# A third place for forward states, output scales in half the steps, a later last transpose and earlier latent norms in a hybrid retention and attention layer

## The chip, the cores and the metric

The kernel runs on one core of one Trainium2 chip. A core has TensorE (PE, matmuls and transposes into PSUM), VectorE (DVE), ScalarE (ACT), GpSimd (POOL) and SyncE (SP, which here issues nearly all DMAs). Each engine works through its own instructions in order and waits on semaphores for the others. The metric is the time of one execution in microseconds (us) on the device; lower is better. Before the change it was 2648.01 us, the median of three runs (2645.45 to 2649.12).

## The reference

One layer of a diffusion transformer over 2048 latent tokens of width 1024 and 256 context tokens, all in float32. What is computed, cut to what matters:

```python
h  = modulate(rmsnorm(x, norm1_g), sh1, sc1)           # latents
hc = modulate(rmsnorm(ctx, norm1_g), csh1, csc1)       # context
rq, rk, rv, rg, aq, ak, av = split(h @ w_in)           # 2816 columns
s_f, s_b = final states of the context's keys and values, forward and backward
# retention: 4 heads of 128, chunks of 128 tokens, both directions
state = state * c_dec + (k * k_dec).T @ v              # from chunk to chunk
ret = group_norm(o_forward + o_backward) * gn_g * silu(rg)
# attention: 8 query heads over 2 key heads of 64, keys of context and latents
att = softmax(q @ k.T / 8) @ v
x = x + g1 * (concat(ret, att) @ w_out)
h2 = modulate(rmsnorm(x, norm2_g), sh2, sc2)
x = x + g2 * (square(relu(h2 @ w_ff1)) @ w_ff2)        # hidden width 4096
return rmsnorm(x, final_norm_g)
```

## The kernel before, in words

Every float32 product is made of three half-precision products: each operand is split into a high and a low part ("hi", "lo"; ScalarE makes the high part, VectorE or GpSimd subtracts it), and hi times hi, hi times lo and lo times hi are summed in PSUM. The kernel has three stages, and in each of them the order of the instructions on every engine is written out by hand.

**Projections** (to about 604 us). The work is a list of units, one for each block of columns of w_in and each token tile (128 tokens): 24 matmuls (lines 1192 to 1194) into one of five PSUM tiles of the pool psO. Everything else is put beside the units with `do(step, part, function)`: after the matmuls of unit s, `run_step(s)` issues the functions put at step s, in the order of PARTS (hi, evac, turned, low, vec, pool, root, aux, turn, load, store). The evacuation of unit s - 1 stands in part evac of step s. Group 0 of the tiles is the context and four latent tiles; the other twelve latent tiles (group 1) are read and normalised beside the units of group 0. Each such tile has a step b: its load (line 450) is at b - 4, its square with a sum along the row (line 457, ScalarE) at b - 2, the root of the mean (lines 461 and 462, GpSimd) at b - 1, the multiplication by the root (norm, line 466, VectorE) and the eight transposes (line 480, TensorE, into two tiles of the PSUM pool psT, which has two) at b. The scaling that reads them (line 485, VectorE) and the shift (line 489, GpSimd) are at b + 1, the high part (line 492) at b + 2, the low part (line 495) at b + 3. The tile's place in SBUF is one of six and is free after the low part. L541 is the low part of a weight block. The first unit of the block RV has the step 20, so b runs from 23 to 28 and from 30 to 35.

**Attention and retention** (about 604 to 1485 us). Step k of `on(k, phase, function)` runs the phases begin, scores, piece, maximum, early, exp, cast, low, chain, pe, values, late, dma. For each step TensorE makes one tile of scores (line 210), one piece of the row maxima's scores (line 177 or 181, two PSUM tiles; VectorE reduces them at line 190 one step later) and some of the products with the values (lines 243 and 245). Beside it run the retention and, one tile of 128 tokens after the other from the last to the first, the output projection. `retention(26)` first takes the forward state from chunk 12 on: for each of five chunks a product of weighted keys and values (line 1633, two steps; GpSimd weighs the keys at line 1627, both operands are loaded ahead by SyncE) and an update of the state (line 1643, VectorE, in phase late). Each state goes to DRAM by line 1648. The states are written to tiles with the tag "sf", of which there are two; the backward states that follow have the tag "sb", of which there are two as well. `output_scales(39)` makes the scales of the output projection: a maximum over a column (VectorE), a transpose (TensorE), a maximum, a product that spreads it over the partitions (TensorE), and nine small VectorE operations, one list entry at each of eight steps in phase late. They set gns (read at the roots of the retention's group norm from step 53 on), sco and inv (read from step 67 on).

**Feed-forward** (from about 1485 us). One level of Strassen's scheme makes seven products do for eight, of sums and differences of blocks; an item is one of the seven: twelve matmuls (lines 2071 to 2073) into a PSUM tile from a ring of six tiles, evacuated by VectorE (line 2083) or ScalarE (line 2093). The last output tile (tokens 0 to 127) is finished at the join of the stages: x1 is stored (line 1850), normalised in place by GpSimd (`norm`, line 1860), transposed (line 1865, eight transposes into the two banks of psX), modulated by VectorE (line 1870), shifted by GpSimd (line 1875) and stored as h2 (line 1878). From `transpose_x` on these eight calls lie in the list `rest`, and the loop over items at the end takes two of them after the matmuls of each item, from the first item on. When the list is empty, psX is closed and its two banks join the ring as its next two tiles. In this join the seven h forms (line 2061), and raw weights (line 2030) are loaded; sums of weights are made by GpSimd (line 2042), their high and low parts by ScalarE (line 2047) and VectorE (line 2053).

Of the kernel before, what the change touches and what calls it, by code (L numbers as in the profile page):

```python
# [41 lines left out]
STATES = 12  # L42
# [14 lines left out]
def layer_kernel(ctx: ExitStack, tc: tile.TileContext, a: dict, out: bass.AP):  # L57
# [70 lines left out]
    def binade(x):  # L128

        nc.vector.tensor_scalar_max(x, x, 1e-15)  # L130
        nc.vector.tensor_single_scalar(x.bitcast(I32), x.bitcast(I32), 0x7F800000, op=ALU.bitwise_and)
# [17 lines left out]
    class Group:  # L149
# [52 lines left out]
        def turn(self):  # L202
            for i in range(0, P, 32):
                nc.vector.transpose(self.qr[64:96, 1, :, i : i + 32], self.mt[i : i + 32])
# [65 lines left out]
    with ExitStack() as st, tc.manual_schedule():  # L270
# [36 lines left out]
        def do(s, part, fn, *args):  # L307
            steps.setdefault((s, part), []).append((fn, args))
# [188 lines left out]
        def new_h(g, kind, i):  # L497
            if g == 0:
                return [hp.tile([P, KT, P], F32R, name=f"h{v}_{kind}{i}", tag="h") for v in ("hi", "lo")]
            h = hp.tile([P, 2, KT, P], F16, name=f"h_{kind}{i}", tag="h")  # L500
            return [h[:, 0], h[:, 1]]
# [705 lines left out]
        for (g, col), w in weights.items():  # L1207
            s = first[g, col]
# [3 lines left out]
            for j in range(w.n):  # L1212
                f, h = s - 5 + j, s - 3 + j if j < 2 else s - 1
                if (g, col) == (0, C_AQ):
                    f, h = s - 7 + j, s - 4 + j
                if (g, col) == (1, C_RQ):
                    f, h = s - 9 + j, (s - 6, s - 5, s - 2, s - 2)[j]
                f, h = f - early_by, h - early_by
# [3 lines left out]
        for n, (col, s) in enumerate(((C_RK, 5), (C_AKV, 6), (C_AQ, 12), (C_RQ, 16), (C_RV, 18), (C_RG, 26))):  # L1222
            w = weights[0, col]
            for j in range(w.n):
                at = s + (j if col != C_RV else j > 0)
                to = 1536 + 4 * n if col != C_RG else 1560
# [5 lines left out]
        for n, tile_of in enumerate(GROUPS[1]):  # L1232
            b = first[0, C_RV] + 3 + n + n // 6
            rows, x = Rows([tile_of], 1), {}

            def turn(n=n, rows=rows, x=x):
                kind, i = GROUPS[1][n]
                hs[1, n] = new_h(1, kind, i)
                x["p"] = [Part(kind, rows.x[0], hs[1, n], k, 4) for k in (0, 4)]
                for p in x["p"]:  # L1240
                    p.turn()

            def each(what, x=x):
                for p in x["p"]:
                    getattr(p, what)()

            do(b - 4, "load", rows.load, 0)
            do(b - 2, "hi", rows.square, 0)
            do(b - 1, "hi", rows.root)
            do(b, "vec", rows.norm, 0)  # L1250
            do(b, "turn", turn)
            do(b + 1, "vec", each, "scale")
            do(b + 1, "pool", each, "shift")
            do(b + 2, "hi", each, "high")
            do(b + 3, "low", each, "low")
# [15 lines left out]
        s = first[1, C_RG]  # L1271
# [222 lines left out]
        s = len(units)  # L1494
# [9 lines left out]
    def pool(stack, name, bufs=1, **kw):  # L1504
        return stack.enter_context(tc.tile_pool(name=name, bufs=bufs, reuse_waits="tile", **kw))
# [23 lines left out]
    def bank(i, shape=(P, 4, P)):  # L1529
        return psX.tile(list(shape), F32, name=f"bank{i}", tag=f"bank{i}")  # L1530
# [3 lines left out]
    def on(k, phase, fn, *args):  # L1534
        events.setdefault((k, phase), []).append((fn, args))

    def run(k, phase):
        for fn, args in events.pop((k, phase), ()):
            fn(*args)
# [4 lines left out]
    def link():  # L1544
        if chain:
            chain.pop(0)()
# [63 lines left out]
    def retention(k0):  # L1610
# [94 lines left out]
        for n, (d, c) in enumerate(todo):  # L1705
            k = k0 + SF * n
            on(k - 7, "dma", take, c, "rk")
            on(k - 5, "dma", take, c, "rv")
            on(k - 3, "late", weigh, d, c)
            on(k, "pe", product, c, n % 2, (0, 1))  # L1710
            on(k + 1, "pe", product, c, n % 2, (2, 3))
            if d == 0:
                old, to, tag = ("f" if c == STATES else "s", c - 2), ("s", c - 1), "sf"
            else:
                old, to, tag = None if c == 1 else ("b", NT), ("b", NT - 1 + c), "sb"
            on(k + 1, "late", update, d, c, old, to, tag, (0, 1))
            on(k + 2, "late", update, d, c, old, to, tag, (2, 3))
            if d == 0:
                on(k + 2, "dma", keep_state, c - 1)
        assert k0 + SF * len(todo) <= R0  # L1720
        for n in range(NT):
            c, k = NT - 1 - n, R0 + RF * n
# [24 lines left out]
    rest = []  # L1747

    def rest_steps(n):
        for _ in range(min(n, len(rest))):  # L1750
            fn, *args = rest.pop(0)
            fn(*args)
# [6 lines left out]
    def output_scales(k):  # L1759

        x = {}

        def greatest():
            w = vp.tile([P, P + 4], F32, name="os")
            x["y"], x["t"], x["one"], x["m"] = w[:, :1], w[:, 1:2], w[:1, 4 : 4 + P], w[:1, 2:3]
            nc.vector.memset(x["one"], 1.0)
            nc.vector.tensor_reduce(x["y"], wmx[:, 72:], axis=AX.X, op=ALU.max, apply_absolute_value=True)

        def turn():
            x["ps"] = bank(1)  # L1770
            nc.tensor.transpose(x["ps"][:1, 0], x["y"], ident)

        def whole():
            nc.vector.tensor_reduce(x["m"], x["ps"][:1, 0], axis=AX.X, op=ALU.max)

        def spread():
            x["ps"] = bank(1)
            mm(x["ps"][:, 0, :1], x["one"], x["m"], start=True, stop=True)

        def scales():  # L1780
            y, t, mul = x["y"], x["t"], nc.vector.tensor_scalar_mul
            later = [
                lambda: nc.vector.tensor_copy(y, x["ps"][:, 0, :1]),
                lambda: binade(y),
                lambda: nc.vector.tensor_scalar(y, y, 2.0**-10, inv, op0=ALU.mult, op1=ALU.max),
                lambda: mul(gns[:, 0:1], y, y),
                lambda: mul(gns[:, 1:2], gns[:, 0:1], EPS),
                lambda: mul(sco, sci[:, 7:8], y),
                lambda: nc.vector.reciprocal(t, y),
                lambda: mul(inv, inv, t),  # L1790
            ]
            for i, fn in enumerate(later):
                on(k + 4 + i, "late", fn)

        on(k, "early", greatest)
        on(k + 1, "pe", turn)
        on(k + 2, "early", whole)
        on(k + 3, "pe", spread)
        on(k + 3, "late", scales)
# [153 lines left out]

    done = attention()
    retention(26)
    output_weights(30)
    output_scales(39)
    for n, t in enumerate(range(NT - 1, -1, -1)):
        made_at = output_tile(t, R0 + RF * n, n == NT - 1)
    for j in range(4):  # L1960
# [264 lines left out]
    def up_jobs():  # L2225

        first = {}
        for j, (n, i, hf) in enumerate(JOBS):
            first.setdefault((n, i), j)
            for k in range(4):  # L2230
                on(j, "pe", up_part, n, i, hf, k)
            on(j, "out", up_out, j, n, i, hf)
        for n in range(len(ITEMS) - 1):
            for i in range(7):
                if (n, i) in first:
                    at = first[n, i] + len(ITEMS[n][1]) - 1
                    on(at, "hi", hi_w1, n + 1, i)
                    on(at + 1, "lo", lo_w1, n + 1, i)
            on(first.get((n, 0), 0), "dma", fetch_w1, n + 2)
            if n > 0:  # L2240
                for i in range(2):
                    on(first[n - 1, 5 + i], "sum", sum_w1, n + 1, i)
                    on(first[n, i], "sum", sum_w1, n + 1, 2 + i)
        on(0, "late", lambda: last3[0](0))
        on(20, "late", lambda: nc.scalar.activation(ff["fg"], ff["fg"], AF.Copy, scale=float(D) ** 0.5))
        for j in range(4):
            h_forms(5 + 10 * j, j)
        first1 = first[AHEAD, 0]
        for m, b in enumerate(PLACE):
            w2_forms(first1 + 1 + (8 * m if m < 14 else 11 * m - 32), b)  # L2250
        for i in range(7):
            on(first[NB, 0] + 2 + 2 * i, "dma", fetch_w2, 0, i)
# [155 lines left out]
    with tc.manual_schedule():  # L2408
        for k in range(min(events)[0], max(events)[0] + 1):
            for phase in PHASES:  # L2410
                run(k, phase)
                if phase in ("maximum", "low", "late"):
                    link()
        assert not events and not chain
        up_jobs()
        down_jobs()
        k = min(events)[0]
        while events:
            for phase in FPHASES:
                run(k, phase)  # L2420
                if phase == "pe" and rest:
                    rest_steps(2)
                    if not rest:
                        banks.close()
                        ff["ps"].extend(pool(late_ff, "fp3", space=PSUM), "p", 2)
            k += 1
# [60 lines left out]
```

## Time and profile before

| what | us |
|---|---|
| median of three runs | 2648.01 |
| the profiled execution, whole | 2648.93 |
| its span, first to last instruction | 2647.1 |
| TensorE busy in the span | 2597.4 |
| VectorE busy | 2048.4 |
| GpSimd busy | 1756.4 |
| ScalarE busy | 1504.0 |
| mean granted clock of TensorE | 0.997 |

A line of a timeline has the start and the duration in us, the engine, the line of the kernel, the operation, what it writes and reads, and the number of instructions merged; in brackets stands how long the engine sat idle before it and what ended that. "SPq" is SyncE's queue of DMA issues. In the lists of waits the three numbers are the sum in us, the number of waits and the longest. A line of the windows has the stretch, its length, the busy time of each engine with its instructions, the clock that TensorE was granted (1.00 is full speed), the share of the DMA engines and GB/s. A line of the chain of waits has only start, duration and what it was. Matmuls are pipelined: their durations overlap, and one of 0.38 us is followed by the next after 0.22 us.

### The profile page before, as it was taken

The numbers are of one execution on the slowest core, as the hardware profiler recorded it, in microseconds if no ns is written. First come the engines' busy times: TensorE is split into PE (matmuls) and PEld (weight loads), VectorE is DVE, ScalarE is ACT, GpSimd is POOL, SyncE is SP. The second block draws the span as 40 slices with busy tenths as digits, with TensorE's granted clock in tenths as the row PEclk, the third lists the DMA queues.
The fourth block names the chain that finished last, engine by engine and source line by source line (L and its number), as shares of the span: only waits on it lengthen the run. The fifth ranks groups of instructions, "written<-read, shape, count | busy, mean of one in ns | idle before, by whom it ended". The sixth has DMA issues, their size and how long they took to land.

```text
span 2647.1 us, 45439 instructions
## 1 busy us (share of the span) xinstructions
PE 2597.4 (98%) x16617; PEld 1452.3 (55%) x16617; DVE 2048.4 (77%) x3098; ACT 1504.0 (57%) x2544; POOL 1756.4 (66%) x1451
## 2 busy tenths in 40 slices
PE   8999999998999999999999999999999999999998
PEld 5875555545666666666666444444444444444443
DVE  5788898667888888888887697889886656656686
ACT  3855343426877777888788576666665322222243
POOL 3644566545676668798887685677662666666686
PEclk9999999999999999999999999999999999999999
DMA  7876999737112123333322755777685757475453
GB/s 235 270 253 211 309 325 322 261 116 221 51 57 73 57 85 100 95 85 107 112 81 77 278 160 151 236 237 230 211 291 148 278 174 296 163 288 178 157 189 113
DMA packets 332903, 481.84 MB, mean 182 GB/s; under 512 B 90228, under 2 KB 200068, under 8 KB 328200
## 3 DMA queue, kind: packets, MB, share of 16 engines
q1 hardware_dynamic: 332664, 478.94, 54.9%
q8 instruction: 130, 2.13, 0.3%
q14 instruction: 93, 0.76, 0.1%
q10 hardware_dynamic: 16, 0.01, 0.0%
HBM read 321.89 MB, written 156.38 MB: 181 GB/s over the span
## 4 chain that ended last, share of the span: by engine, by line
PE 82%; DVE 6%; DMA 4%; ACT 4%; issue 2%; POOL 2%; SPq 0%; ACTq 0%; DVEq 0%; POOLq 0%
PE pd L2298 7%; PE pd L2300 7%; PE pd L2299 7%; PE pu L2071 7%; PE pu L2073 7%; PE pu L2072 7%; PE st L210 4%; PE o L245 4%; PE st L211 4%; PE pso L1193 4%; PE pso L1192 4%; PE pso L1194 4%; PE mp L177 3%; PE o L243 2%; PE bank L1835 2%; PE bank L1833 2%
## 5 line engine op out<-in xcount | busy, mean ns | idle before, releaser
L190 DVE TENSOR_REDUCE nm<-mp 128x1 f32<-128x512 f32 x558 | 377.5, 685 | 88.6 <-PE mp L177 82.9
L216 ACT ACTIVATE p<-st 128x512 f32<-128x512 f32 x576 | 341.4, 600 | 158.4 <-PE st L211 154.8
L227 POOL TENSOR_TENSOR plo<-p,phi 128x1024 f16<-128x1024 f32 x160 | 347.7, 2178 | 84.9 <-ACT phi L220 84.8
L2071 PE MATMUL pu<-hf,w1f 128*128 128x512 f16 x896 | 339.8, 379 | 0.6 <-DVE u L1870 0.6
L2072 PE MATMUL pu<-hf,w1f 128*128 128x512 f16 x896 | 339.8, 379 | 0.0
L2073 PE MATMUL pu<-hf,w1f 128*128 128x512 f16 x896 | 339.8, 379 | 0.0
L2298 PE MATMUL pd<-w,uf 128*128 128x512 f16 x896 | 339.6, 379 | 0.0
L2299 PE MATMUL pd<-w,uf 128*128 128x512 f16 x896 | 339.6, 379 | 0.0
L2300 PE MATMUL pd<-w,uf 128*128 128x512 f16 x896 | 339.6, 379 | 0.0
L2318 POOL TENSOR_TENSOR y<-y,d 128x512 f32<-128x512 f32 x128 | 210.4, 1646 | 146.9 <-ACT uf L2287 100.1
L220 ACT ACTIVATE phi<-p 128x1024 f16<-128x1024 f32 x288 | 305.2, 1060 | 0.0
L229 DVE TENSOR_TENSOR plo<-p,phi 128x512 f16<-128x512 f32 x256 | 237.6, 929 | 21.8 <-ACT phi L220 9.4
L243 PE MATMUL o<-wv,plo 128*128 128x65 f16 x2304 | 230.6, 193 | 0.0
L245 PE MATMUL o<-wv,phi 128*128 128x129 f16 x2176 | 228.9, 220 | 0.0
L210 PE MATMUL st<-qr,ks 128*128 128x512 f16 x576 | 218.3, 379 | 10.3 <-ACT p L216 7.9
L243 PEld LDWEIGHTS <-plo 128*128 128x128 f16 x2304 | 205.5, 98 | 29.3 <-issue 1.5
L2310 DVE SCALAR_TENSOR_TENSOR y<-pd,scy,y 128x512 f32<-128x512 f32 x160 | 116.8, 747 | 131.5 <-PE pd L2300 131.5
L211 PE MATMUL st<-qr,ks 128*128 128x512 f16 x576 | 218.5, 379 | 0.0
L2083 DVE TENSOR_TENSOR r<-pu,r 128x512 f32<-128x512 f32 x224 | 149.9, 683 | 82.8 <-PE pu L2073 57.7
L1192 PE MATMUL pso<-wf,h_l 128*128 128x512 f16 (+1 forms) x576 | 208.1, 361 | 0.0
L1194 PE MATMUL pso<-wf,h_l 128*128 128x512 f16 (+1 forms) x576 | 208.1, 361 | 0.0
L1193 PE MATMUL pso<-wf,h_l 128*128 128x512 f16 (+1 forms) x576 | 208.1, 361 | 0.0
(392 smaller groups left out, 6110.4 us busy)
## 6 DMA issues: line engine op xcount, KB each, us to landing
wm<-in_w_ff SPq DMA_DIRECT2D x64, 512.0 KB, 7.1
u<-r SPq DMA_DIRECT2D x128, 256.0 KB, 4.5
ur<-u SPq DMA_DIRECT2D x128, 256.0 KB, 5.8
y<-x SPq DMA_DIRECT2D x64, 512.0 KB, 6.0
wf<-w2f SPq DMA_DIRECT2D x112, 256.0 KB, 3.0
w<-wf SPq DMA_DIRECT2D x28, 1024.0 KB, 10.2
w1r<-in_w_ff SPq DMA_DIRECT2D x48, 512.0 KB, 5.4
x<-y SPq DMA_DIRECT2D x48, 512.0 KB, 2.6
```

The costliest lines, as they stand in the source:

```text
L190: nc.vector.tensor_reduce(dst, src, axis=AX.X, op=ALU.max, negate=True)
L211: mm(ps, ks2[:, self.g, k], q[:, 1], start=False, stop=True)
L216: nc.scalar.activation(self.p[kt // 2][:, kt % 2], self.s.pop(kt), AF.Exp, scale=HD**-0.5)
L227: nc.gpsimd.tensor_tensor(lo, p, hi, op=ALU.subtract)
L243: mm(o[:, : HD + 1], lo[:, i, c], v[:, : HD + 1], start=False, stop=False)
L245: mm(o, hi[:, i, c], v[:, :VW], start=False, stop=last)
L2071: mm(pu[hf, i], whi, hi, start=k == 0, stop=False)
L2072: mm(pu[hf, i], whi, lo, start=False, stop=False)
L2073: mm(pu[hf, i], wlo, hi, start=False, stop=k == 3)
L2298: mm(ps, u[:, 0, b], w[:, b, 0], start=b == 0, stop=False)
L2299: mm(ps, u[:, 0, b], w[:, b, 1], start=False, stop=False)
L2300: mm(ps, u[:, 1, b], w[:, b, 0], start=False, stop=b == 3)
```

## The change

Four places are edited; no operation is added or taken away.

- The twelve latent tiles of group 1: square, root and norm each come one step sooner (b - 3, b - 2, b - 1); load and transposes stay.
- The third of the five forward states (n == 2) is written to a tile with the tag "sb" instead of "sf".
- The output scales start at step 38 instead of 39, and their eight list entries of small operations stand two to a step.
- The calls in `rest` for the last output tile start after the matmuls of the third item (k == 2) instead of the first. So the transposes, the modulation, the shift and the store all come two items later, and so does the joining of the two banks to the ring.

```diff
-            do(b - 2, "hi", rows.square, 0)
-            do(b - 1, "hi", rows.root)
-            do(b, "vec", rows.norm, 0)
+            do(b - 3, "hi", rows.square, 0)
+            do(b - 2, "hi", rows.root)
+            do(b - 1, "vec", rows.norm, 0)
             do(b, "turn", turn)
...
             if d == 0:
-                old, to, tag = ("f" if c == STATES else "s", c - 2), ("s", c - 1), "sf"
+                old, to, tag = ("f" if c == STATES else "s", c - 2), ("s", c - 1), "sb" if n == 2 else "sf"
...
             for i, fn in enumerate(later):
-                on(k + 4 + i, "late", fn)
+                on(k + 4 + i // 2, "late", fn)
...
-    output_scales(39)
+    output_scales(38)
...
                 run(k, phase)
-                if phase == "pe" and rest:
+                if phase == "pe" and rest and k > 1:
                     rest_steps(2)
                     if not rest:
                         banks.close()
```

## The prediction

> **What bounds the kernel now.** I read the page's busy times first, then TensorE's own waits, then the windows with their clock, then the timelines around the longest waits and the chain of waits there.
>
> ```profile
> PE 2597.4 (98%) x16617; PEld 1452.3 (55%) x16617; DVE 2048.4 (77%) x3098; ACT 1504.0 (57%) x2544; POOL 1756.4 (66%) x1451
> ```
>
> TensorE is busy for 98% of 2647.1 us. The change takes no matmul away, so it can only win TensorE's idle 49.7 us (2647.1 - 2597.4) and stretches in which its clock is low.
>
> ```profile
> PE bank L1865 <- POOL xr L1860: 3.1, 1, 3.1
> PE mp L181 <- DVE wmx L190: 2.7, 1, 2.7
> ...
> PE psx L480 <- DVE x_l L466: 2.2, 2, 2.0
> PE psx L711 <- ACT sq L659: 2.1, 1, 2.1
> ...
> PE mp L177 <- DVE wmx L190: 0.6, 1, 0.6
> PE pu L2071 <- DVE u L1870: 0.6, 1, 0.6
> ```
>
> The columns are the sum, the number of waits and the longest. The three waits of 2.0 to 3.1 us each stand where one edit acts: L480 is the latents' transposes, L181 (with 0.6 at L177) waits for maxima that stand behind the state updates on VectorE, L1865 is the last tile's transposes, with 0.6 behind them at L2071. Next, the windows: length, busy time of each engine, then the granted clock.
>
> ```profile
> 180.00:200.00 20.00, 19.26 (x90) 16.21 (x91) 18.12 (x20) 15.69 (x26) 12.93 (x13) 0.91 0.49 159
> 360.00:380.00 20.00, 16.07 (x93) 8.72 (x92) 15.94 (x23) 8.22 (x14) 8.52 (x12) 1.00 0.94 319
> ...
> 620.00:640.00 20.00, 16.70 (x150) 12.00 (x148) 16.72 (x36) 10.76 (x17) 14.38 (x13) 0.91 0.82 263
> ```
>
> ```profile
> 1450.00:1500.00 50.00, 44.72 (x272) 23.07 (x271) 21.28 (x30) 20.82 (x38) 27.18 (x26) 0.97 0.73 274
> ```
>
> The clock falls in these three windows with 0.91, 0.91 and 0.97, and the three waits lie in them. It costs 0.09 x 20 = 1.8, again 1.8, and 0.03 x 50 = 1.5 us. The window at 360, with the wait of 2.1 us at L711, keeps 1.00. So a wait of two to three microseconds may, but need not, cost nearly its own length again:
>
> ```profile
> 178.35 0.39 PE L1194 MATMUL pso<-whi,hlo_l 128*128 128x512 f32 x1
> 180.74 1.48 PE L480 MATMUL psx<-ident,x_l 128*128 128x128 f32 x8 [2.00 <-DVE x_l L466]
> ...
> 184.15 0.63 PE L1194 MATMUL pso<-whi,hlo_l 128*128 128x512 f32 x1
> ...
> 188.07 0.39 PE L1192 MATMUL pso<-whi,hhi_l 128*128 128x512 f32 x1
> ```
>
> After the wait a matmul takes 0.63 us, later 0.39. What the three places lose in all: 2.0 + 1.8 = 3.8 (latents), 0.6 + 2.75 + 1.8 = 5.15 (states), 3.1 + 0.6 + 1.5 = 5.2 (last tile); 14.2 us is the most the change can win.
>
> [...]
>
> **The change part by part.**
>
> *Latents a unit sooner.* In each of 12 tiles a square (ScalarE), two small root operations (GpSimd) and one norm (VectorE) move one unit ahead; no DMA moves. The third tile decides:
>
> ```profile
> 174.76 3.50 DVE L541 TENSOR_TENSOR wlo<-wst,whi 128x1024 fp32r<-128x1024 f32 x3 [6.09 <-PE pso L1194]
> 178.18 1.28 DVE L485 TENSOR_TENSOR x_l<-psx,a 128x512 f32<-128x512 f32 x2
> 179.38 1.22 DVE L466 TENSOR_SCALAR x_l<-x_l,xy 128x1024 f32<-128x1024 f32 x1
> ```
>
> VectorE sits idle for 6.09 us, then takes three weight splits, two scalings (L485) and the norm, and TensorE starts at 180.74, 2.00 us late. One unit sooner the norm of 1.2 us falls into that idle stretch. What is late next are the two scalings: they free the two PSUM tiles (psT has two) that the transposes write, and they end at 178.8 and 179.46, where TensorE is ready at 178.7 (178.35 + 0.39). The first four transposes take some 0.4 us (estimate, half of the slow eight's 1.48 at full clock), so about 0.6 us of wait is left. The fourth tile's norm takes the vacated place, so nothing behind it moves. Gain 3.8 - 0.6 = 3.2 us. Ends: 1.4 if the clock falls in any case, 3.8 if nothing is left. The square's load stays where it is, so ScalarE may now wait for it, with evacuations queued behind; priced as a rival.
>
> *Third place.* No instruction is added.
>
> ```profile
> 617.66 0.61 DVE L1643 SCALAR_TENSOR_TENSOR sf<-sf,cd,bank 128x128 f32<-128x128 f32 x2 [1.63 <-DMA sf<-sf]
> ...
> 623.45 0.60 DVE L1643 SCALAR_TENSOR_TENSOR sf<-sf,cd,bank 128x128 f32<-128x128 f32 x2 [1.54 <-DMA sf<-sf]
> ...
> 627.39 0.61 DVE L1643 SCALAR_TENSOR_TENSOR sf<-sf,cd,bank 128x128 f32<-128x128 f32 x2 [1.62 <-DMA sf<-sf]
> ```
>
> The third, fourth and fifth update each wait for the store of the state two before them; behind them on VectorE stand the maxima for which TensorE waits. With "sb" for the third, the first of these waits goes, and the fourth finds its place (stored by 617.66) free. The fifth now needs the second state's place, whose store landed at 623.45. So VectorE reaches the fifth update at 623.45 instead of 627.39: 3.9 us sooner. The "sb" place comes back for the second backward state, by when its store has long landed. What is late on TensorE next is the load of the sixth product's v:
>
> ```profile
> 620.87 0.38 SPq L1619 DMA_DIRECT2D orv<-rv  x1
> ```
>
> ```profile
> 626.73 1.04 POOL L1627 TENSOR_TENSOR okw<-ork,kd 128x512 f32<-128x512 f32 x1 [2.85 <-DMA ork<-rk]
> ```
>
> ```profile
> 624.71 0.38 PE L181 MATMUL mp<-ks,qr 128*128 128x256 f16 x2 [2.75 <-DVE wmx L190]
> ...
> 628.32 0.65 PE L1633 MATMUL bank<-orv,okw 128*128 128x128 f32 x4
> ```
>
> The load behind it in the queue landed at 626.73; one transfer of 256 KB earlier, this one lands at about 625.8 (estimate). TensorE took that product at 628.32, so it wins only 2.5 us here. VectorE's lead of 3.9 us then takes some of the next wait, 1.16 us at 642.68 (row below): I take 0.7. Gain 3.2 us; ends 1.0 (loads later still, or the clock falls in the new wait of about 2 us) and 5.15.
>
> *Output scales.* The first operations come one step sooner, the nine small ones of VectorE that follow in four steps, not eight. Nobody waits for them: the first root that reads gns comes eight steps later, the first part scaled by inv some twenty. But they now stand ahead of a late maximum:
>
> ```profile
> 641.88 0.15 DVE L1783 COPY os<-bank 128x1 f32<-128x1 f32 x1
> ```
>
> ```profile
> 642.68 0.38 PE L177 MATMUL mp<-ks,qr 128*128 128x512 f16 x1 [1.16 <-DVE nm L190]
> ```
>
> One of them (0.15 us) stood ahead of it, now five: up to 0.6 us if VectorE is still behind, nothing if the third place has put it ahead. I take 0.3 us of loss.
>
> *Last tile's transposes.* Eight transposes pass two items (24 matmuls), two modulations pass four or five operations on VectorE, two shifts pass a sum on GpSimd, two stores pass loads on SyncE (read back some thirty items later), and the two freed banks join the ring two items later.
>
> ```profile
> 1474.17 13.37 DMA x<-xr
> 1487.80 1.10 POOL xr L1860
> ...
> 1500.29 0.22 PE pu L2072
> ```
>
> ```profile
> 1488.96 1.97 PE L1865 MATMUL bank<-ident,xr 128*128 128x128 f32 x8 [3.10 <-POOL xr L1860]
> ...
> 1499.91 0.38 PE L2071 MATMUL pu<-hf,w1f 128*128 128x512 f16 x1 [0.64 <-DVE u L1870]
> ```
>
> ```profile
> 1494.74 0.98 DVE L2053 SCALAR_TENSOR_TENSOR w1f<-w1s,sc,w1f 128x512 f16<-128x512 f32 x1 [3.65 <-ACT w1f L2047]
> ...
> 1497.98 1.28 DVE L2083 TENSOR_TENSOR r<-pu,r 128x512 f32<-128x512 f32 x2
> 1499.18 1.27 DVE L1870 TENSOR_TENSOR u<-bank,a 128x512 f32<-128x512 f32 x2
> 1500.38 1.15 DVE L2053 SCALAR_TENSOR_TENSOR w1f<-w1r,sc,w1f 128x512 f16<-128x512 f32 x1
> ...
> 1504.13 0.68 DVE L2083 TENSOR_TENSOR r<-pu,r 128x512 f32<-128x512 f32 x1
> ```
>
> The last tile is normalised in place, so GpSimd waits 13.37 us for its store to land (the queue is full of loads). TensorE's wait of 3.10 us is covered by two items of 2.6 us each (12 matmuls, 0.22 us of the chain each). But GpSimd stays held until 1487.80, and all that hangs on it stays where it was: the weights of the fifth item are split at 1494.74 to 1495.72, and the bank for the sixth is freed by the second sum at 1497.98, so at 1499.26. TensorE is ready at 1488.96 - 3.10 = 1485.9, runs items two and three to 1491.0, transposes for 0.8 us (estimate as above), runs item four to 1494.4, waits a good microsecond in item five, ends it at 1497.95, starts item six at 1499.35 and ends it at 1501.95. Item seven needs a freed bank, that is the first modulation, now behind the four groups from 1500.38 to 1504.81: without the modulations ahead of them they end at about 1503.6, and the bank is free at 1504.3 (1503.1 if GpSimd gets in the way less). Before, item seven started at 1499.91 + 5.2 = 1505.1. So 0.8 to 2.0 us are left of 5.2; a fallen clock after the new waits would take up to 1.5. I take 0.9; ends -0.7 and 5.2.
>
> **Sum.** -3.2 - 3.2 + 0.3 - 0.9 = -7.0 us. The profiled execution took 2648.93 us, so 2641.9; it lay 0.9 above the median of 2648.01, so I forecast **2641.0**.
>
> **The rivals.**
> *The last tile pays in full.* If VectorE has caught up by the new place, 5.2 instead of 0.9: 2641.0 - 4.3 = 2636.7. For it: the wait at L1865 is the longest. Against: the chain of 13.37 us is not shortened.
> *The loads take the stores' place.* The third place gives 1.0, the last tile loses 0.5: 3.2 + 1.0 - 0.5 - 0.3 = 3.4, so 2644.6. For it: the wait of 2.85 us for ork at 626.73.
> [...]
> *Slower: ScalarE blocks on the latents' loads.*
>
> ```profile
> x_l<-in_x SPq DMA_DIRECT2D x1, 512.0 KB, 5.6
> ```
>
> ```profile
> 208.61 0.33 SPq L450 DMA_DIRECT2D x_l<-in_x  x1
> ```
>
> ```profile
> 210.31 1.06 ACT L457 ACTIVATE junk<-x_l 128x1024 bf16<-128x1024 f32 x1
> ```
>
> The load at 208.61 is the eleventh tile's; its square now comes about where the tenth's stood, 210.31. At 5.6 us to landing that holds ScalarE 3.9 us. Six tiles load into a reused place: 6 x 3.9 = 23.4 us; all of it on TensorE gives 2641.0 + 23.4 = 2664.4. It decides once evacuations are later than psO's five banks bear, some four units of 24 matmuls, over 5 us each, which 3.9 is far from.
>
> **How the numbers follow.** A measurement of this kernel can tell about 0.2%, 5.3 us, from no change. Chances: forecast 0.53 (own range 2638.5 to 2643.5), last tile in full 0.15, loads 0.15, slow clock 0.13, slower 0.04. Faster by over 0.2% (below 2642.7): 0.43 + 0.15 + 0.04 + 0.02 = 0.64; within: 0.32; slower: 0.04. Range 2636.0 to 2647.0: both ends of the unknown costs without the slower rival and the last bit of the fastest.
>
> **What would show it.** Right: no wait at L480 for L466 and a clock of 1.00 around 180; no wait of L1643 at the third update, a shorter one at the fifth, and a new wait of TensorE for orv; L1860 still released by the store of x1, no wait at L1865, but new waits at L2071 for r and u. Wrong: the fifth update still waits as long; L2071 runs through; squares that hold TensorE's banks.

## The result and the profile after

The changed kernel took 2642.48 us in the median of 20 runs (2638.81 to 2647.13), the kernel before 2646.79 us in the median of 20 (2643.51 to 2650.13): a ratio of 0.9985, 95% interval 0.9979 to 0.9991, so 4.0 us less (2.4 to 5.6). A second comparison, with 11 and 15 runs, gave 2642.30 against 2647.23 us, a ratio of 0.9976 (0.9967 to 0.9985), 6.4 us less (4.0 to 8.7). All 31 and 35 runs together have medians of 2642.45 and 2647.22 us, 4.8 us apart, which is 0.18%. The forecast was 2641.0 us, 7.0 us less, with a range of 2636.0 to 2647.0. The time lies in the range and the direction is right. Both intervals leave out zero, so the change is a gain. By the prediction's own bound of 0.2% it counts as no change in the first comparison (0.15%), to which the prediction gave 0.32, and as faster in the second (0.24%), to which it gave 0.64.

The profiled execution took 2639.86 us, with a span of 2638.0, which is 9.1 us less than the span before. That is no measure of the change: it lies 2.6 us below the median of its kernel, and the one before lay 2.1 us above its own. So each part is read first in this one pair of profiles, and then in fourteen.

The busy time of TensorE, from the page after (the engines' busy times):

```profile
PE 2595.5 (98%) x16617; PEld 1449.8 (55%) x16617; DVE 2045.0 (78%) x3098; ACT 1504.4 (57%) x2544; POOL 1761.0 (67%) x1451
```

It sits idle for 2638.0 - 2595.5 = 42.5 us, before for 49.7. TensorE's waits in the changed kernel (sum, number, longest):

```profile
PE pu L2071 <- DVE u L1870: 2.9, 1, 2.9
...
PE mp L181 <- DVE wmx L190: 0.7, 1, 0.7
...
PE bank L1633 <- DMA orv<-rv: 0.6, 2, 0.4
PE pu L2071 <- DVE r L2083: 0.6, 1, 0.6
...
PE pu L2073 <- DVE w1f L2053: 0.4, 1, 0.4
...
PE psx L480 <- DVE x_l L485: 0.3, 1, 0.3
...
PE pu L2071 <- ACT w1f L2047: 0.2, 1, 0.2
```

The 2.7 us at L181 have become 0.7 and the 2.0 us at L480 have become 0.3. The 3.1 us at L1865 are gone from the list, but in their place stand 2.9, 0.6, 0.4 and 0.2 us a few items later, 4.1 us together. The windows of the changed kernel (length, busy time of each engine, granted clock, DMA share, GB/s):

```profile
180.00:200.00 20.00, 20.00 (x104) 16.78 (x104) 19.73 (x22) 15.75 (x26) 15.48 (x13) 1.00 0.50 159
360.00:380.00 20.00, 18.08 (x105) 10.49 (x104) 16.64 (x25) 8.97 (x17) 11.64 (x15) 0.91 0.95 324
620.00:640.00 20.00, 19.10 (x199) 14.08 (x197) 19.28 (x49) 13.58 (x22) 14.60 (x14) 1.00 0.90 314
1480.00:1500.00 20.00, 15.85 (x76) 7.24 (x75) 14.74 (x18) 13.34 (x23) 16.47 (x13) 1.00 0.73 240
```

The three slow stretches of before are at full clock here. The stretch at 360, where the change touches nothing, is slow instead: 0.91 where before had 1.00.

**Latents.** The timeline of the changed kernel:

```profile
180.00 1.23 PE L480 MATMUL psx<-ident,x_l 128*128 128x128 f32 x8 [0.27 <-DVE x_l L485]
...
212.13 1.06 ACT L457 ACTIVATE junk<-x_l 128x1024 bf16<-128x1024 f32 x1 [3.56 <-DMA x_l<-in_x]
...
218.33 1.06 ACT L457 ACTIVATE junk<-x_l 128x1024 bf16<-128x1024 f32 x1 [2.63 <-DMA x_l<-in_x]
```

As forecast, the norm no longer holds the transposes; the scalings at L485 do, for 0.27 us. ScalarE does block on the loads, for 3.56 and 2.63 us, as the slower rival said. TensorE has no wait there: it is busy for all 14.00 us from 208 to 222, with the five banks of psO between it and ScalarE.

**States.** The same kernel's timeline around the state updates:

```profile
613.59 0.60 DVE L1643 SCALAR_TENSOR_TENSOR sb<-sf,cd,bank 128x128 f32<-128x128 f32 x2
...
618.07 0.59 DVE L1643 SCALAR_TENSOR_TENSOR sf<-sb,cd,bank 128x128 f32<-128x128 f32 x2
...
620.30 0.59 DVE L1643 SCALAR_TENSOR_TENSOR sf<-sf,cd,bank 128x128 f32<-128x128 f32 x2
...
624.86 0.68 PE L1633 MATMUL bank<-orv,okw 128*128 128x128 f32 x4 [0.25 <-DMA orv<-rv]
```

No update waits for a store any more, not even the fifth (620.30), which the prediction had wait until the second state had landed. The new wait for orv is there, with 0.25 us.

**Last tile.** The same kernel's timeline at the join:

```profile
1479.38 1.12 POOL L1860 TENSOR_SCALAR xr<-xr,cy_f 128x1024 f32<-128x1024 f32 x1 [11.64 <-DMA w1r<-in_w_ff]
...
1482.54 1.04 PE L1865 MATMUL bank<-ident,xr 128*128 128x128 f32 x8
1486.39 0.39 PE L2071 MATMUL pu<-hf,w1f 128*128 128x512 f16 x1 [0.22 <-ACT w1f L2047]
1487.40 0.39 PE L2073 MATMUL pu<-hf,w1f 128*128 128x512 f16 x1 [0.41 <-DVE w1f L2053]
1490.34 0.38 PE L2071 MATMUL pu<-hf,w1f 128*128 128x512 f16 x1 [0.60 <-DVE r L2083]
...
1495.28 1.27 DVE L1870 TENSOR_TENSOR u<-bank,a 128x512 f32<-128x512 f32 x2
...
1496.01 0.38 PE L2071 MATMUL pu<-hf,w1f 128*128 128x512 f16 x1 [2.92 <-DVE u L1870]
```

The transposes run without a wait, but GpSimd is held for 11.64 us as before, and TensorE waits in item five (1486.39 and 1487.40), before item six (1490.34) and before item seven (1496.01): at the three points that the prediction named. The row of L1860 puts its wait down to the load of w1r; but that instruction reads only xr and its scale and writes xr, so what it needs is the store of x1, which SyncE issues at 1465.83, just ahead of that load (the profile of before has this wait, 13.37 us, under "x<-xr").

### The profile page after: what moved, and what is told of

The parts are those of the page before. It is cut to its first block, busy times and chain, and to the rows that moved or that the text cites. A ratio compares the mean times of both kernels' runs of the same rounds, so it can differ in the third digit from the quotient of the medians.

```text
span 2638.0 us, 45431 instructions
## 1 busy us (share of the span) xinstructions
PE 2595.5 (98%) x16617; PEld 1449.8 (55%) x16617; DVE 2045.0 (78%) x3098; ACT 1504.4 (57%) x2544; POOL 1761.0 (67%) x1451
## 3 DMA queue, kind: packets, MB, share of 16 engines
q8 instruction: 130, 2.13, 0.3%
## 4 chain that ended last, share of the span: by engine, by line
PE 69%; ACT 3%; POOL 2%; DVE 1%; DMA 1%; issue 1%; DVEq 0%; POOLq 0%; ACTq 0%; SPq 0%
PE pd L2300 7%; PE pd L2298 7%; PE pd L2299 7%; PE pu L2071 7%; PE pu L2073 7%; PE pu L2072 7%; PE st L210 4%; PE o L245 4%; PE st L211 4%; PE mp L177 3%; PE o L243 2%; PE bank L1835 2%; PE bank L1833 2%; PE bank L1834 2%; ACT p L216 1%; ACT phi L220 1%
## 5 line engine op out<-in xcount | busy, mean ns | idle before, releaser
L2071 PE MATMUL pu<-hf,w1f 128*128 128x512 f16 x896 | 339.6, 379 | 3.7 <-DVE u L1870 2.9
L2073 PE MATMUL pu<-hf,w1f 128*128 128x512 f16 x896 | 339.6, 379 | 0.4 <-DVE w1f L2053 0.4
L2298 PE MATMUL pd<-w,uf 128*128 128x512 f16 x896 | 339.6, 379 | 0.0
L210 PE MATMUL st<-qr,ks 128*128 128x512 f16 x576 | 218.0, 379 | 10.3 <-ACT p L216 7.9
```

The lines of the kernel that those rows point to most:

```text
L2071: mm(pu[hf, i], whi, hi, start=k == 0, stop=False)
L2073: mm(pu[hf, i], wlo, hi, start=False, stop=k == 3)
L2298: mm(ps, u[:, 0, b], w[:, b, 0], start=b == 0, stop=False)
```

## How the fourteen profiles are compared

TensorE's program has the same instructions at the same marks in every kernel here, so a stage is measured between two starts. These are the marks in the third profile of the changed kernel (timeline rows):

```profile
166.53 0.66 PE L711 MATMUL psx<-ident,ys 128*128 128x128 f32 x4 [0.37 <-DVE x_l L485]
368.40 0.44 PE L837 MATMUL psx<-ident,kn 128*128 128x128 f32 x2 [2.00 <-DVE ks L842]
605.04 0.38 PE L210 MATMUL st<-qr,ks 128*128 128x512 f16 x1 [1.45 <-ACT p L216]
651.88 0.38 PE L177 MATMUL mp<-ks,qr 128*128 128x512 f16 x1 [0.27 <-DVE nm L190]
1466.73 0.66 PE L1865 MATMUL bank<-ident,xr 128*128 128x128 f32 x4 [0.52 <-DVE xr L1840]
2052.66 0.38 PE L2298 MATMUL pd<-w,uf 128*128 128x512 f16 x1
```

"Latents" is from L711 to L837, less the wait that ends it (2.00 here; it is 1.2 to 2.1 in all kernels and nothing of this change). "States" is from L210 to L177, "last tile" from L1865 to L2298. Between L177 and L1865 all fourteen take 814.85 to 815.01 us, and from L2298 to the end 587.71 to 587.80: nothing of the difference lies there. Two stretches stand in no column: from the start to L711 (164.83 to 166.53 us) and from L837 to L210 (234.85 to 238.08, with a mean of 236.15 in the profiles with the latents' edit and 236.31 in those without). They differ from execution to execution, so the spans in the table differ by more than its columns. The last column names the windows of 20 us from 100 us on, up to 2600, in which the clock was below 0.95.

| profile | span | latents | states | last tile | clock below 0.95 |
|---|---|---|---|---|---|
| before | 2647.1 | 203.09 | 53.05 | 585.15 | 180, 620, 1480 |
| before, again | 2641.5 | 201.45 | 50.34 | 584.87 | 1480 |
| latents alone | 2641.6 | 199.89 | 51.20 | 585.15 | none |
| states alone | 2639.0 | 201.44 | 46.43 | 585.05 | 1480 |
| scales alone | 2647.5 | 203.08 | 51.26 | 586.02 | 180, 1480 |
| last tile alone | 2645.9 | 201.45 | 51.13 | 586.57 | 360, 620, 1500 |
| last tile alone, again | 2641.4 | 201.44 | 50.74 | 584.01 | none |
| after | 2638.0 | 199.90 | 46.96 | 584.40 | 360 |
| after, again | 2639.7 | 199.86 | 47.27 | 586.01 | 1480 |
| after, third | 2640.4 | 199.87 | 46.84 | 585.93 | 1480 |
| late loads | 2634.1 | 199.90 | 47.55 | 582.04 | none |
| late loads, again | 2637.5 | 199.84 | 49.77 | 581.40 | none |
| late loads, old place | 2633.2 | 199.85 | 46.19 | 581.51 | 360 |
| late loads and late gains | 2635.1 | 199.86 | 47.10 | 580.72 | none |

## The experiments

After the result two theories stood against each other. Theory A: the clock falls by chance, so a removed wait is worth about its own length. Theory B: the fall belongs to the wait and goes with it, as the prediction's terms had it. Four kernels make one edit each.

**Latents alone.** The kernel before with this edit:

```
-            do(b - 2, "hi", rows.square, 0)
-            do(b - 1, "hi", rows.root)
-            do(b, "vec", rows.norm, 0)
+            do(b - 3, "hi", rows.square, 0)
+            do(b - 2, "hi", rows.root)
+            do(b - 1, "vec", rows.norm, 0)
```

> The kernel before with the latents' norm one unit sooner, and nothing else. Theory A (the clock falls by chance, in one execution at one place and in the next at another, so a removed wait is worth its own length): the wait of 2.00 us at 180 becomes 0.3 to 0.6, so -1.4 to -1.7 us. Theory B (the fall of the clock belongs to the wait, and goes with it): 1.8 us more, so -3.2 us, and the time of this kernel no longer spreads by the clock. The profile should show no wait at L480 for L466.

It took 2644.85 us in the median of 11 runs, the kernel before 2647.01 in the median of 35: ratio 0.9991 (0.9983 to 1.0), so 2.4 us less (0 to 4.5). That holds both theories' numbers. The profile says more (timeline of this kernel):

```profile
178.74 1.23 PE L480 MATMUL psx<-ident,x_l 128*128 128x128 f32 x8 [0.27 <-DVE x_l L485]
...
1483.39 1.09 PE L1865 MATMUL bank<-ident,xr 128*128 128x128 f32 x8 [3.06 <-POOL xr L1860]
...
1494.39 0.38 PE L2071 MATMUL pu<-hf,w1f 128*128 128x512 f16 x1 [2.13 <-DVE u L1870]
```

The wait at L480 went, as it should. But this profile has a wait of 3.06 us at L1865, and behind it full clock: its eight transposes take 1.09 us, at a low clock 1.97, and no window is below 0.95. Theory B, in which each such wait brings its fall, does not hold.

**States alone.** The kernel before with this edit:

```
-                old, to, tag = ("f" if c == STATES else "s", c - 2), ("s", c - 1), "sf"
+                old, to, tag = ("f" if c == STATES else "s", c - 2), ("s", c - 1), "sb" if n == 2 else "sf"
```

> The kernel before with the third forward state in the other ring, and nothing else. The prediction gave -3.2 us, at most -5.15. The profile of the changed kernel showed more: TensorE's waits between 606 and 660 fell from 6.0 to 1.8 us, and the store of the second state itself came 3.7 us sooner. Theory A: -3.9 us if all of that is this edit's own, -2.5 if the last three of those waits (1.8 us together) need the output scales' edit too. Theory B: 1.8 us more, -4.3 to -5.7. The profile should show no update at L1643 that waits for a store.

2642.23 us in the median of 12 runs: ratio 0.9984 (0.9976 to 0.9993), 4.2 us less (1.9 to 6.4). By the table the stage takes 46.43 us, where the four kernels with the old places, in six profiles, take 50.34 to 53.05. So this edit alone does all that the change does there. The second state's store is issued 1.0 us after its update ended (613.96), where the first trace of before had it 2.2 us after (615.42), behind two loads that held SyncE for 3.46 us; in this trace they held it for 2.10. SyncE's queue in this kernel, and then in the kernel before:

```profile
614.95 0.42 SPq L1648 DMA_DIRECT2D sf<-sf  x1
```

```profile
613.65 3.46 SPq L1619 DMA_DIRECT2D ork<-rk  x2
...
617.64 0.42 SPq L1648 DMA_DIRECT2D sf<-sf  x1
```

**Scales alone.** The kernel before with this edit:

```
-                on(k + 4 + i, "late", fn)
+                on(k + 4 + i // 2, "late", fn)
...
-    output_scales(39)
+    output_scales(38)
```

> The kernel before with the output scales in half the steps, one step sooner, and nothing else. The prediction gave +0.3 (0 to 0.6) us, by small operations ahead of a late maximum. Rival: it is what moves the maxima at 636 and 642 and the product at 643 (1.8 us of TensorE's waits), and so saves up to 1.8 us of itself. Both theories on the clock give the same here: the wait of 2.75 us before it stays.

2648.73 us in the median of 11 runs: ratio 1.0005 (0.9996 to 1.0013), 1.3 us more (1.1 less to 3.4 more), so nothing that can be told. In the profile one wait grew (timeline of this kernel; 1.16 us before):

```profile
642.08 0.38 PE L177 MATMUL mp<-ks,qr 128*128 128x512 f16 x1 [1.88 <-DVE nm L190]
```

The stage as a whole takes 51.26 us, like the others of the old kind. The small operations do stand ahead of a late maximum, as the prediction said, and the price is within what the stage varies. The rival that this edit removes the waits at 636 to 643 has fallen: they are there.

**Last tile alone.** The kernel before with this edit:

```
-                if phase == "pe" and rest:
+                if phase == "pe" and rest and k > 1:
```

> The kernel before with the last tile's transposes two steps later, and nothing else. The prediction gave -0.9 us (5.2 to be had, the rest given back in new waits). Theory A: the two waits of before (3.10 and 0.64 us, together 3.7) stand against new ones of 4.2 us, so +0.4 us on average, or no change that can be told. Theory B: the slow stretch after the 3.10 us goes too, so -0.9 us or a little more. The profile should show GpSimd still held at L1860 by the store of x1, no wait at L1865, and waits at L2071 of about 4 us together.

2647.32 us in the median of 11 runs: ratio 1.0000 (0.9991 to 1.0008). Its profile has the new waits (0.25, 0.42, 0.60 and 3.36 us at L2071 and L2073, 4.6 together) and a slow window after them:

```profile
1500.00:1520.00 20.00, 17.75 (x75) 7.73 (x75) 20.00 (x22) 15.72 (x28) 18.10 (x13) 0.91 0.68 209
```

This edit wins nothing. The four sums of single edits are 2.4 + 4.2 - 1.3 + 0.0 = 5.3 us, near the 4.0 and 6.4 us that were measured for all together.

**The changed kernel and the kernel before, once more.**

> The changed kernel once more. For the time: 2642.5 us, ratio 0.9985. For the clock, theory A (falls come by chance): stretches below full clock in this profile lie at other places than in the first one (there 0 and 360 us). Theory B (bound to waits): at the same places, and none at 180, 620 and 1480.

> The kernel before once more, one look. Theory A: of the three places where the clock was below 1.00 (180, 620, 1480) one or two are now at full clock, though the waits of 2.0, 2.4 to 2.75 and 3.1 us are there as before. Theory B: all three again.

The time came to 2642.30 us (ratio 0.9976, above). Of the kernel before, this one execution took 2643.26 us. Its windows and its two waits:

```profile
180.00:200.00 20.00, 19.25 (x98) 16.26 (x99) 19.67 (x21) 16.68 (x28) 14.48 (x14) 1.00 0.50 159
...
1480.00:1500.00 20.00, 16.48 (x74) 8.03 (x73) 12.03 (x15) 9.65 (x16) 16.00 (x13) 0.91 0.68 227
```

```profile
180.75 1.06 PE L480 MATMUL psx<-ident,x_l 128*128 128x128 f32 x8 [2.00 <-DVE x_l L466]
...
1483.28 1.97 PE L1865 MATMUL bank<-ident,xr 128*128 128x128 f32 x8 [2.79 <-POOL xr L1860]
...
1494.26 0.38 PE L2071 MATMUL pu<-hf,w1f 128*128 128x512 f16 x1 [0.73 <-DVE u L1870]
```

The same wait of 2.00 us at L480 now has full clock behind it. And the changed kernel now falls at 1480, where its first profile did not. So the fall is a matter of the execution. Yet it is no free chance either. By the table, of six profiles with the wait at L480 two fell at 180, and of eight without it none did. Of six with the old places of the states two fell at 620, of eight with the third place none. With the old place of the transposes four of five fell at 1480, with the new one three of five. At 360, with a wait of 1.2 to 2.1 us at L837 in every kernel, three of fourteen did. A fall comes behind a wait, but only in a part of the executions: theory A has the size right and B the place.

Narrow windows show a fall by itself. Here is the clock (third number from the end) around the same wait of 2.00 us at L480, in the first profile of before and then in states alone:

```profile
177.83:181.24 3.41, 1.41 (x9) 0.93 (x9) 3.41 (x5) 0.89 (x2) 2.23 (x2) 1.00 0.00 0
181.24:184.66 3.42, 3.42 (x13) 2.83 (x11) 3.38 (x6) 3.14 (x7) 1.83 (x3) 0.50 0.00 0
184.66:188.07 3.41, 3.41 (x17) 2.77 (x15) 3.41 (x4) 2.36 (x4) 3.19 (x4) 1.00 0.86 265
```

```profile
177.00:180.41 3.41, 1.97 (x9) 1.31 (x7) 3.41 (x5) 1.42 (x4) 1.17 (x2) 1.00 0.00 0
180.41:183.82 3.41, 2.84 (x17) 2.53 (x18) 3.37 (x5) 2.59 (x5) 2.89 (x3) 1.00 0.00 0
```

In before the wait ends at 180.74, and from 181.24 on the clock is 0.50 for 3.41 us, which takes 1.7 us of TensorE's time. The other two falls of this profile read 0.50 for 3.41 us as well, from 624.98 and from 1488.55 on; the waits they belong to end at 624.71 and 1488.96. In states alone the wait at L480 is as long, and the clock is 1.00 through it and behind it. Nor does the length decide elsewhere: a wait at L837 of 1.92 us brought a fall in the first profile of the changed kernel, one of 2.00 us there brought none in its third (rows of the marks above), nor did the 3.06 us at L1865 in latents alone. So the fall belongs to a wait, as theory B has it, but what decides in which execution it comes was not shown.

What a fall costs depends on what stands behind it. At 180 it costs 203.09 - 201.45 = 1.6 us. At 1480 in the old place it costs nothing: the stage took 585.15, 584.87 and 585.05 us with a clock of 0.91, and 585.15 in the one profile without a fall (586.02 in scales alone, where the window shows 0.83). The second profile of before and that of latents alone (rows above) show why. With transposes at a low clock (1.97 us) TensorE then waits 0.73 us for u, at full clock (1.09 us) 2.13 us: VectorE's chain from L1860 on sets the end of that wait either way. In the new place the wait for u before item seven comes last, and nothing behind it hides a slow stretch.

**What a fall costs in the new place.**

> The changed kernel a third time, one look. From the transposes of the last tile's first half (L1865) to the first matmul of the last stage (L2298) the kernels with the old place took 584.9 to 585.2 us whether the clock fell there or not (586.0 once, at 0.83); with the new place 584.4 without a fall and 586.0 and 586.6 with one. Theory: in the old place a slow stretch lies before TensorE's wait for VectorE and is hidden by it; in the new place the last wait (3 us, at item seven) has nothing behind it that hides a slow stretch. So this run takes 584.4 +-0.2 if no window between 1480 and 1520 is below 0.95, and 585.8 to 586.6 if one is. Rival: the difference is noise of the loads, and does not go with the clock.

> The kernel before with the last tile's edit alone, once more, one look. The same as for the changed kernel: 584.4 us between those two points without a fall of the clock, 585.8 to 586.6 with one. The waits at L480 and L181 are there as before, with a fall behind each in about two of five profiles so far.

The changed kernel fell (windows), with slow matmuls from item seven on (timeline), and took 585.93 us for the stage; the time was 2642.19 us:

```profile
1480.00:1500.00 20.00, 15.98 (x69) 6.92 (x68) 13.73 (x17) 12.61 (x21) 16.41 (x13) 0.92 0.72 242
```

```profile
1496.74 0.58 PE L2071 MATMUL pu<-hf,w1f 128*128 128x512 f16 x1 [2.63 <-DVE u L1870]
```

The last tile's edit alone did not fall and took 584.01 us; 2643.17 us in all:

```profile
1480.00:1500.00 20.00, 16.24 (x77) 7.38 (x76) 11.13 (x15) 9.98 (x17) 13.70 (x11) 1.00 0.84 281
1500.00:1520.00 20.00, 20.00 (x94) 9.07 (x93) 20.00 (x19) 14.63 (x26) 19.92 (x14) 1.00 0.67 212
```

```profile
1499.37 0.38 PE L2071 MATMUL pu<-hf,w1f 128*128 128x512 f16 x1 [2.67 <-DVE u L1870]
```

Both came as expected, the second 0.2 us below its bound. In the new place two profiles without a fall have a mean of 584.2 us, three with one of 586.2. By these means a fall costs 2.0 us here; 1.6 to 1.8 of them are the slow stretch itself (0.92 and 0.91 in windows of 20 us), and where the rest comes from is not shown.

**Loads behind the store.** If GpSimd's hold bounds the last tile, the store of x1 has to come ahead of some of the 7 MB of loads that stand before it in SyncE's queue. The changed kernel, with three of the seven hf loads issued after the store and the loads of w1r:

```
-            on(k0 + i // 2, "dma", fetch_h, i)
+            on(k0 + i // 2 if i < 4 else made_at + 2 + (i - 4) // 2, "dma", fetch_h, i)
```

> The changed kernel with the last three of the seven loads of 1 MB (hf) moved behind the store of x1 and the loads of w1r on SyncE's queue; nothing else differs. Theory (the last tile's gain is bounded by GpSimd, held 11.6 us at L1860 by that store behind the loads): L1860 starts at about 1470 instead of 1479, TensorE's waits at L2071 for w1f, r and u (4.2 us together) go, and the median falls by about 4 us below that of the changed kernel, to 2638 or 2639. Rival (VectorE and ScalarE are the bound there, GpSimd only the name in the row): L1860 starts sooner, but 2 to 3 us of these waits stay, and the gain is 1 to 2 us. Second rival: the moved loads come too late for items five to seven, and TensorE waits for hf.

> The run with late loads once more, for the comparison: 2636 to 2638 us; the wait for hf of about 2 us at 1475.

2636.15 us in the median of 5 runs, ratio 0.9954 (0.9942 to 0.9967), and in the next comparison 2638.45 us in 6 runs, 0.9968 (0.9956 to 0.998). The timeline of the first:

```profile
1469.84 1.12 POOL L1860 TENSOR_SCALAR xr<-xr,cy_f 128x1024 f32<-128x1024 f32 x1 [3.63 <-DMA w1r<-in_w_ff]
...
1475.48 0.38 PE L2071 MATMUL pu<-hf,w1f 128*128 128x512 f16 x1 [2.07 <-DMA hf<-hf]
```

GpSimd starts 5.5 us after the mark at L1865 (1464.34) instead of 13.5 (1479.38 after 1465.86), and none of the four new waits is left. The stage takes 582.04 and 581.40 us, 3.7 us less than the changed kernel's 585.45 (mean of three profiles). So the theory holds, and the second rival with it: the fifth hf is now 2.07 us late.

The same with the transposes in their old place (without `k > 1`):

> As the run before, but with the last tile's transposes back in their old place (before the second item, not the third). Theory: with GpSimd free the wait of 3.1 us at L1865 does not come up, so the old place costs nothing and both kernels take the same time, 2638 to 2639; the later transposes were a way around the store, no gain of their own. Rival: the later place wins 0.4 to 0.7 us of itself, by letting two items run ahead of the modulations.

2639.23 us in 5 runs, ratio 0.9962 (0.995 to 0.9975), an interval that overlaps with that of the run before; the stage takes 581.51 us against 582.04 and 581.40. The transposes run in the old place without a wait:

```profile
1477.40 1.04 PE L1865 MATMUL bank<-ident,xr 128*128 128x128 f32 x8
```

With the store out of the way the stage shows no cost of the old place.

**Two more loads moved.** The late loads, with g2b and fgb behind them:

```
-        nc.sync.dma_start(ff["g2"], gate_d[1].partition_broadcast(P))
...
-        nc.sync.dma_start(ff["fg"], a["final_norm_g"].partition_broadcast(P))
...
+        on(made_at + 4, "dma", lambda: nc.sync.dma_start(ff["g2"], gate_d[1].partition_broadcast(P)))
+        on(made_at + 4, "dma", lambda: nc.sync.dma_start(ff["fg"], a["final_norm_g"].partition_broadcast(P)))
```

> As the run with late loads, with the two loads of 512 KB (g2b and fgb), which nobody reads before some 40 us later, moved behind the hf loads too. In the run with late loads TensorE waited 2.07 us for the fifth hf at 1475.5. Theory (the queue's bytes ahead of it are the bound: it carries some 0.4 MB a us here, so 1 MB less is 2.4 us): this wait goes, L1860 starts some 2 us sooner, and TensorE has no wait between 1466 and 1490; 2 us below the run with late loads, 2634. Rival: the fifth hf waits for its issue on SyncE behind w1r, not for bytes, and the wait stays.

2636.90 us in 5 runs, ratio 0.9961 (0.9949 to 0.9974); the late loads in the same comparison 2638.45. The timeline:

```profile
1471.42 1.12 POOL L1860 TENSOR_SCALAR xr<-xr,cy_f 128x1024 f32<-128x1024 f32 x1 [2.93 <-DMA x<-xr]
...
1476.58 0.38 PE L2071 MATMUL pu<-hf,w1f 128*128 128x512 f16 x1 [0.87 <-DMA hf<-hf]
```

The wait for hf fell from 2.07 to 0.87 us, the stage to 580.72 us: half of what the count of bytes gave. GpSimd starts 4.8 us after the mark (1466.63) instead of 5.5, so 0.7 us sooner and not 2. The stage is the shortest of all, though its median cannot be told from that of the other kernels with late loads. All four medians with late loads (2636.15 to 2639.23) lie below those of the changed kernel (2642.30 and 2642.48), though some of the intervals overlap.

## Why the prediction was right or wrong

- **Direction, range and places: right.** L480 waits for L485 and no longer for the norm, the new wait for orv came, the new waits of the last tile came in item five, before item six and before item seven. That the time came within 1.5 us of the forecast owes something to luck: the latents and the last tile were put 1.1 and 1.0 us too high, the states 0.8 too low, and the forecast started from 2648.01, where the kernel before took 2646.79 in the comparison, which moved it 1.2 us nearer.
- **Latents: -3.2 forecast; mechanism right, size too large.** The step that failed is the 1.8 us of slow clock, taken whole into what the place loses ("2.0 + 1.8 = 3.8"). Without a fall the edit wins 201.45 - 199.87 = 1.6 us, with one 3.2, and two of six profiles with the wait had one: 1.6 + 0.33 x 1.6 = 2.1 us. The run of this edit alone gave 2.4.
- **Third place: -3.2 forecast, 4.0 us by the means of six and eight profiles (51.29 and 47.26), 4.2 by the run.** The size was near, the working was not. "The fifth now needs the second state's place, whose store landed at 623.45" took that landing as fixed. But its store was issued at 617.64 only because SyncE had been held by the loads of ork ahead of it, 3.46 us in that execution. In the other five profiles with the old places the hold is 1.5 to 2.2 us, and the wait of 1.63 us at the third update is 0 to 0.79. The one trace of before was an odd one here: 53.05 us against 50.34 to 51.26 in the other five. What came on top is that the waits at 636.06, 642.68 and 643.37 (1.8 us) went with it, of which the prediction took 0.7. The 1.8 us of slow clock in this place's 5.15 are not shown: last tile alone had a fall there and took 51.13 us, latents and scales alone had none and took 51.20 and 51.26. The gain isn't safe: in one of the eight profiles with the third place the loads of v were late twice, a wait of 1.65 us came up at L177, and the stage took 49.77 us. Why the loads were late there stays open.
- **Output scales: +0.3 forecast, nothing that can be told.**
- **Last tile: -0.9 forecast, 0.1 us of loss by the means of five and five profiles (585.25 and 585.38).** Up to item seven the step was right: in the new place it starts 29.75 to 30.63 us after the mark at L1865, in the old one 1505.1 - 1474.2 = 30.9 (30.6 to 30.9 in three others, 31.8 in scales alone, whose window shows 0.83). The step that failed is the slow clock, twice. The prediction counted 1.5 us of it in what the place loses, and it cost nothing there, since the wait for u hid it. And it kept the clock up after the new waits ("a fallen clock after the new waits would take up to 1.5"), where in three of five profiles it fell and took 2.0 us.
- **Sum.** 2.1 + 4.0 - 0.1 = 6.0 us by the stages, 4.0 and 6.4 us in the two comparisons. The forecast's 7.0 came from one profile in which all three places had their slow stretch; none of the other thirteen profiles has a fall at all three.
- **Rivals.** That the clock stays slow (0.13) was right about half: the fall is not owed by each wait, as the prediction's reading of one trace had it. The wait of 2.00 us at L480 brought one in two of six profiles, and so did the wait at L181. The prediction priced the fall seen in one trace as if every execution had it. "The last tile pays in full" fell; late loads show what it would have needed. "The loads take the stores' place" fell for the states (4.0 us, not 1.0) and came near at the last tile (0.1 us of loss, it had 0.5). Of "Slower" the blocked ScalarE came, and no wait of TensorE with it.

## What to carry to other kernels

Whether the clock falls behind a short wait differs from execution to execution: here the same wait of 2.00 us at L480 brought a fall in two of six profiles, and the waits at the last tile brought one in seven of ten. So price it by the share of profiles that show it, and only where nothing later would absorb the lost time. Before an engine's wait is covered by moving work, look at what holds the engine that releases it; here a 512 KB store behind 7 MB of loads held GpSimd for 11.6 us, moving three loads won 3.7 us, and moving the work around it won nothing. One profile is one draw: where stages start and end at fixed instructions, measure them between these marks in several profiles, as the spread of single executions (10 us here) is larger than the change.

## What the runs showed of the hardware

- The 31 executions of the changed kernel differ by up to 9.9 us (2637.25 to 2647.13). The profiles place such differences: 1.6 us at L480 where its wait stands, 3.6 us in the states' stage with the third place (46.19 to 49.77), 2.6 us at the last tile with the new place (584.01 to 586.57), 3.2 us between L837 and L210 (234.85 to 238.08) and 1.7 us ahead of L711, while the 815 us from there to the last tile vary by 0.16 and the last 588 us by 0.09.
- The clock fell behind waits of 1.92 to 3.36 us, in three of fourteen to four of five profiles at a place, and at L480, at L181 and at the last tile in none without the wait. In the first profile of before each of the three falls reads 0.50 for 3.41 us. A window of 20 us that holds a fall shows 0.91 or 0.92, once 0.83.
- With the queue full (DMA share 1.02, 387 GB/s from 1465.8 to 1479.4 in the changed kernel), a 512 KB store issued behind 8 MB of loads (seven hf, g2b, fgb) let GpSimd go 13.5 us after its issue, behind 5 MB 5.6 us after (late loads, again), and behind 4 MB 4.8 us after (late loads and late gains).
